# Two more PSUM banks for the dense products, and exponential and key transposes queued behind dense tiles, while gate matrices are made

## The chip, the cores and the metric

The kernel runs on one core of a Trainium2 chip. The metric is the device time of one execution in microseconds (us), as the median over several runs. TensorE is PE here (PEld is its weight load), VectorE DVE, ScalarE ACT, GpSimd POOL, and SyncE, whose queue issues most transfers, SP.

## The reference

A trunk of two layers over 512 tokens of width 1024, in float32. Layer 0 mixes by retention, layer 1 by differential attention; each is followed by a PEER expert layer, in which the gates arise:

```
q = (xc @ w_q).reshape(PEER_CHUNK, PEER_HEADS, 2, half)
sc = einsum('thpd,hpnd->thpn', q, subkeys)
s1, i1 = top_k(sc[:, :, 0], 16);  s2, i2 = top_k(sc[:, :, 1], 16)
cand = s1[..., :, None] + s2[..., None, :]      # 256 pairs of each head
top, pos = top_k(cand, 16)
idx  = expert number i1 * 128 + i2 of each chosen pair   # 8 heads x 16
gate = softmax(top)
act  = gelu(u[idx] . xc)
out  = sum over the 128 chosen experts of gate * act * v[idx]
```

There are 128 x 128 = 16384 experts, with rows `u` and `v` of 1024.

## The kernel before, in words

Products that need float32 are made of three passes (`mm3`, L95 to L98): both factors are split into a high part (`wh`, ACT, L92) and a low part (`wl`, L93, on POOL for dense tiles) and high by high, high by low and low by high are summed in PSUM.

The expert layer (`peer`, L868) treats the four blocks of 128 tokens in two ways. Block 0 is sparse: for each of its 128 chosen experts POOL gathers one row of `u` per token by an indirect transfer and DVE takes the dot product (`sparse_u`, L737), later the same with `v` (`sparse_v`, L747). Blocks 1 to 3 (384 tokens) are dense: for each of 128 groups of 128 experts a dense tile (`u_tile`, L843) computes all first products, 8 x 3 matmuls of 384 columns, and ACT takes the GELU out of the bank (L849). Gate matrices, mostly zeros, then weigh the activations, and a second product with `v` is summed over all 128 groups.

There are two stages. In the first, the one that is changed, the gate matrices are made while dense tiles run beside. The steps for a block t of 1 to 3 are:

- `topk_pairs` (L682, DVE alone): the best 16 of the candidate pairs of each head, in eight steps that each give back a cost PC = 2.2. Its last instruction, L728, subtracts the maximum: `tk_g`.
- `softmax` (L730): the exponential on ACT (L731), then sum, reciprocal and product on DVE.
- `gate_rows` (L800): DVE splits the expert number into two keys (`g_if`, L806), PE transposes both keys and the gate into one bank with the tag `rt` (L809), and DVE copies them out (`g_tr`, L811).
- `gmat` (L816): eight chunks of 16 tokens. For each four tokens DVE compares (`g_eq`, L826) and weighs (`g_oh`, L829), ACT converts (L828), PE multiplies two one-hot matrices into a `pj` bank (L833), ACT takes the result out (L836, L838). A chunk gives back a cost of 6.0 and its gates go to DRAM.

A generator, `gates()`, strings these together: the pairs of block t + 1 advance two steps after each chunk of block t, and are finished and followed by `gate_rows` at chunk 5. The loop at L920 adds up the costs that it gives back. Whenever the sum passes the dense tiles' own account, which starts at -40 and grows by UT = 4.0 per tile, it emits a tile and stores its activations to DRAM (L924). After LAG = 22 tiles it also emits sparse dot products, DOTS = 0.6 per tile, each with a cost of 1.2. In the second stage the stored tiles are loaded and weighed, and the tiles that were not made yet are made there.

What is emitted first has the higher priority. A scheduler then fixes one order for each engine before the run, with its own estimate of durations. Every engine keeps its order: an instruction that waits holds up all that stand behind it.

PSUM has eight banks: four with the tag `pj`, two `mu`, two `rt`. Dense tiles use `mu` (L845), so that a tile waits for the GELU of the tile two before it. `wh` and `wl` have three buffers. The second stage adds up in the four `pj` banks and the two `rt` banks. All loads of 128 x 1024, gathers included, go round one ring of nine buffers (`wraw`).

Of the kernel before, what the change touches and what calls it, by code (L numbers as in the profile page):

```python
# [2 lines left out]

# [20 lines left out]
AF = mybir.ActivationFunctionType  # L24
# [4 lines left out]
P = 128  # L29
S = 512  # L30
D = 1024
TB = S // P
KD = D // P
# [10 lines left out]
DT = 384  # L44

GT = 16
# [16 lines left out]
def build(tc, I, out):  # L63
    nc = tc.nc
    ctx = ExitStack()
    with ctx:
# [18 lines left out]
        XTH = xp.tile([P, KD, S], F32R, name="xth")  # L85
        XTL = xp.tile([P, KD, S], F32R, name="xtl")

        def bank(tag):
            return psum.tile([P, 512], F32, name=tag, tag=tag, bufs=4 if tag == "pj" else 2)
# [5 lines left out]
        def mm3(o, ah, al, bh, bl, start, stop):  # L95
            nc.tensor.matmul(o, ah, bh, start=start, stop=False)  # L96
            nc.tensor.matmul(o, ah, bl, start=False, stop=False)  # L97
            nc.tensor.matmul(o, al, bh, start=False, stop=stop)  # L98

        def wload(src, eng=None, pool=None, tag="", bufs=3, dst=None):  # L100
            a = src.shape[1]
            pool = pool or wp
            raw = wp.tile([P, 1024], F32, name="wraw", tag="wraw", bufs=RING)
            nc.sync.dma_start(raw.rearrange("p (a b) -> p a b", a=a), src)
            if dst is None:
                h = pool.tile([P, 1024], F32R, name="wh", tag="wh" + tag, bufs=bufs)
                l = pool.tile([P, 1024], F32R, name="wl", tag="wl" + tag, bufs=bufs)
            else:
                h, l = dst
            split(h, l, raw, eng)  # L110
            return h.rearrange("p (a b) -> p a b", a=a), l.rearrange("p (a b) -> p a b", a=a)
# [29 lines left out]
        def col_unit(b, W, q, c, ts):  # L141
            wh, wl = W
            cs = slice(c * P, c * P + P)
            for k in range(2):
                kk = 2 * q + k
                mm3(b, wh[:, k, cs], wl[:, k, cs], XTH[:, kk, ts], XTL[:, kk, ts], kk == 0, kk == 7)
# [583 lines left out]
        def softmax(gate):  # L730
            nc.scalar.activation(gate, gate, AF.Exp)  # L731
            zs = small.tile([P, 8], F32, name="tk_z", tag="tk_z")
            nc.vector.reduce_sum(out=zs, in_=gate, axis=AX.X)
            nc.vector.reciprocal(out=zs, in_=zs)
            nc.vector.tensor_tensor(out=gate, in0=gate, in1=zs.unsqueeze(2).to_broadcast([P, 8, 16]), op=OP.mult)
# [64 lines left out]
        def gate_rows(kp, idx, gate):  # L800

            ii = kp.tile([P, 2, P], I32, name="g_ii", tag="g_ii")
            nc.vector.tensor_scalar(out=ii[:, 0, :], in0=idx, scalar1=7, scalar2=None, op0=OP.arith_shift_right)
            nc.vector.tensor_scalar(out=ii[:, 1, :], in0=idx, scalar1=127, scalar2=None, op0=OP.bitwise_and)
            fi = kp.tile([P, 2, P], F32, name="g_if", tag="g_if")
            nc.vector.tensor_copy(out=fi, in_=ii)  # L806
            b = bank("rt")
            for i, src in enumerate((fi[:, 0, :], fi[:, 1, :], gate)):
                nc.tensor.transpose(b[:, i * P:i * P + P], src, ident)  # L809
            tr = kp.tile([P, 3, P], F32, name="g_tr", tag="g_tr", bufs=2)  # L810
            nc.vector.tensor_copy(out=tr.rearrange("p a b -> p (a b)"), in_=b[:, :3 * P])  # L811
            ks = kp.tile([P, 2, P], BF16, name="g_ks", tag="g_ks", bufs=2)
            nc.vector.tensor_copy(out=ks, in_=tr[:, 0:2, :])
            return tr, ks
# [25 lines left out]
                nc.sync.dma_start(gd[t0 // GT + q], st.rearrange("p a t -> p (a t)"))  # L840
                yield 6.0

        def u_tile(dp, l, a):  # L843
            uh, ul = wload(I[f"ut{l}"][a], nc.gpsimd)
            b = bank("mu")  # L845
            for k in range(KD):
                mm3(b[:, :DT], uh[:, k, :], ul[:, k, :], XTH[:, k, S - DT:], XTL[:, k, S - DT:], k == 0, k == KD - 1)
            act = dp.tile([P, DT], F32, name="uact", tag="uact", bufs=LEAD + 1)
            nc.scalar.activation(act, b[:, :DT], AF.Gelu_apprx_tanh)  # L849
            return act  # L850

        def v_prep(kp, l, a, act, g):
# [15 lines left out]
        def peer(l, norm, feed, prepare):  # L868
            with tc.tile_pool(name="sp", bufs=1) as sp, tc.tile_pool(name="dp", bufs=1) as dp:
                gd = dram.tile([DT // GT, P, (P - GA * NG0) * GT], F32, name=f"gd{l}")  # L870
# [4 lines left out]
                G0 = [dp.tile([P, DT // GT, GA, GT], F32, name="gl", tag="gl", bufs=2) for _ in range(NG0)]  # L875
                with tc.tile_pool(name="p1", bufs=1) as kp:
                    M = [kp.tile([P, 16, 16], F32, name=f"tk_m{t}") for t in range(TB)]
                    MI = [kp.tile([P, 16, 16], U32, name=f"tk_i{t}") for t in range(TB)]
                    with tc.tile_pool(name="pq", bufs=1) as qp:
                        scores(qp, M, MI, l, norm, feed)  # L880
                        if l == 0:
                            iota_f = qp.tile([P, P], F32, name="iota_f")
                            nc.sync.dma_start(iota_f, I["iota"])
                            nc.vector.tensor_copy(out=iota50,
                                                  in_=iota_f[:, :NCAND].unsqueeze(2).to_broadcast([P, NCAND, 16]))
                            nc.vector.tensor_copy(out=iota4, in_=iota_f.unsqueeze(2).to_broadcast([P, P, 4]))
                    with tc.tile_pool(name="tk", bufs=1) as tp:
                        def pairs(t, got):
                            idx = tp.tile([P, P], I32, name="tk_idx", tag="tk_idx", bufs=2)
                            gate = tp.tile([P, 8, 16], F32, name="tk_g", tag="tk_g", bufs=2)  # L890
                            yield from topk_pairs(tp, M[t], MI[t], idx, gate)
                            softmax(gate)
                            got.append((idx, gate))

                        def gates():

                            got = []
                            yield from pairs(1, got)
                            for t in range(1, TB):
                                rows = nxt if t > 1 else gate_rows(tp, got[0][0], got[0][1].rearrange("p h k -> p (h k)"))  # L900
                                if t + 1 < TB:
                                    more = pairs(t + 1, got)
                                for n, cost in enumerate(gmat(tp, *rows, (t - 1) * P, gd, G0)):
                                    yield cost
                                    if t + 1 < TB:
                                        for _ in range(2):
                                            c = next(more, None)
                                            if c:
                                                yield c
                                        if n == P // GT - 3:  # L910
                                            for c in more:
                                                yield c
                                            nxt = gate_rows(tp, got[-1][0], got[-1][1].rearrange("p h k -> p (h k)"))

                        for _ in topk_pairs(tp, M[0], MI[0], idx0, gate0):
                            pass
                        su = sparse_u(sp, 0, l, idx0, act0)
                        nu, nd, tv, tu = 0, 0, 0.0, -40.0

                        for cost in gates():  # L920
                            tv += cost
                            while tu < tv and nu < P:
                                act = u_tile(dp, l, nu)
                                nc.sync.dma_start(ad[nu], act)  # L924
                                nu += 1
                                tu += UT
                                while nd < DOTS * (nu - LAG):
                                    next(su, None)
                                    nd += 1
                                    tv += 1.2  # L930
                with tc.tile_pool(name="p2", bufs=1) as kp:
# [24 lines left out]
                    for a in range(P):  # L956
# [7 lines left out]
                        if a < nu:  # L964
                            act = kp.tile([P, DT], F32, name="aact", tag="aact", bufs=4)
                            nc.sync.dma_start(act, ad[a])
                        else:
                            act = ahead.pop(0)
# [25 lines left out]
        def to_attention():  # L994
# [5 lines left out]
            return Norm(0, 1), Feed(srcs, nc.gpsimd).fill(3)  # L1000

        nxt = peer(0, *retention(), to_attention)
        peer(1, *attention(*nxt), lambda: (Norm(1, 1, out), None))


# [60 lines left out]
```

## Time and profile before

| | |
|---|---|
| time, median of 3 runs | 3379.78 us (3376.13 to 3380.93) |
| the profiled execution's own time | 3375.29 us |
| its span | 3373.5 us |
| PE busy | 3225.8 us, 96% |
| DVE busy | 2636.5 us, 78% |
| POOL, ACT busy | 1615.7 us and 1393.4 us, 48% and 41% |
| first stage, layer 0 | about 540 to 960 us |
| first stage, layer 1 | about 2150 to 2575 us |

The span runs from the first to the last instruction. An engine that is busy for most of the span may still stand idle where it counts, so the rows are read stage by stage.

### The profile page before, as it was taken

What the parts mean: (1) busy time and instruction counts of PE and PEld (TensorE: products, weight loads), DVE (VectorE), ACT (ScalarE), POOL (GpSimd) and SP (SyncE); (2) the same over time, 40 slices, a digit from 0 to 9 for tenths busy, and PEclk for the clock granted to TensorE, in tenths of its full rate; (3) what the DMA queues carried; (4) which work ended last, traced back from release to release, by engine and by line L of the source; (5) the groups of instructions that cost most, each with busy time, mean ns of one, the idle gap of its engine ahead of it and who ended that gap; (6) DMA issues with size and microseconds to landing.
All of it is one profiled execution on the core that took longest, in us unless ns stands there. A gap on an engine that the chain in (4) does not pass through costs nothing. (4 is left out here: it accounts for less than half of the span.)

```text
span 3373.5 us, 47032 instructions
## 1 busy us (share of the span) xinstructions
PE 3225.8 (96%) x16666; PEld 2863.3 (85%) x16666; DVE 2636.5 (78%) x4593; ACT 1393.4 (41%) x2436; POOL 1615.7 (48%) x919
## 2 busy tenths in 40 slices
PE   9999999789999999999999999978999999999998
PEld 7888889789988889988888668978998888998887
DVE  4444559998868888999873665899986789989996
ACT  3233333476743333333333643337674333333332
POOL 1101335646542357778734423554454224777772
PEclk9999999899999999999999999989999999999999
DMA  5222223566689999899943202346678999989993
GB/s 212 85 85 83 87 94 125 166 210 224 249 295 335 371 327 336 310 334 327 332 145 95 73 26 90 124 151 211 219 249 270 338 346 360 332 321 334 323 330 128
DMA packets 304572, 763.36 MB, mean 226 GB/s; under 512 B 25040, under 2 KB 146256, under 8 KB 304336
## 3 DMA queue, kind: packets, MB, share of 16 engines
q1 hardware_dynamic: 230608, 491.88, 42.8%
q0 software_dynamic: 73728, 268.47, 22.3%
q8 instruction: 131, 2.15, 0.3%
q14 instruction: 105, 0.86, 0.1%
HBM read 687.37 MB, written 72.88 MB: 225 GB/s over the span
## 5 line engine op out<-in xcount | busy, mean ns | idle before, releaser
L93 POOL TENSOR_TENSOR wl<-wraw,wh 128x1024 fp32r<-128x1024 f32 x316 | 847.1, 2684 | 609.6 <-ACT wh L92 567.3
L92 ACT ACTIVATE wh<-wraw 128x1024 fp32r<-128x1024 f32 x632 | 663.6, 1055 | 670.6 <-DMA wraw<-in_ut 143.2
L96 PE MATMUL mu<-xth,wh 128*128 128x384 f32 (+1 forms) x2080 | 712.7, 343 | 40.8 <-ACT uact L849 40.8
L98 PE MATMUL mu<-xth,wl 128*128 128x384 f32 (+1 forms) x2080 | 709.3, 341 | 21.4 <-POOL wl L93 21.4
L97 PE MATMUL mu<-xtl,wh 128*128 128x384 f32 (+1 forms) x2080 | 705.9, 339 | 0.0
L93 DVE TENSOR_TENSOR wl<-wraw,wh 128x1024 fp32r<-128x1024 f32 x316 | 471.8, 1494 | 212.4 <-ACT wh L92 212.1
L741 POOL DMA_INDIRECT ug<-in_u,idx x256 | 309.2, 1208 | 521.6 <-DVE act L743 232.3
L743 DVE CUSTOM_DVE_ANT_0 scr<-ug,x 128x1024 bf16<-128x1024 f32 x256 | 367.4, 1435 | 129.7 <-DMA ug<-in_u,idx 128.7
L96 PEld LDWEIGHTS mu<-xth,wh 128*128 128x128 f32 x2080 | 399.7, 192 | 50.0 <-ACT uact L849 45.6
L92 ACT ACTIVATE wwh<-w 128x384 fp32r<-128x384 f32 x256 | 134.4, 525 | 739.2 <-DVE w L855 407.8
L98 PEld LDWEIGHTS mu<-xth,wl 128*128 128x128 f32 x2080 | 399.3, 192 | 25.5 <-POOL wl L93 25.5
L754 POOL DMA_INDIRECT vg<-in_v,idx x256 | 354.2, 1384 | 131.0 <-DVE x L756 72.4
L756 DVE SCALAR_TENSOR_TENSOR x<-vg,wgt,x 128x1024 f32<-128x1024 f32 x256 | 401.4, 1568 | 5.8 <-DMA vg<-in_v,idx 2.8
L97 PEld LDWEIGHTS mu<-xtl,wh 128*128 128x128 f32 x2080 | 400.0, 192 | 5.0
L97 PE MATMUL pj<-wl,wwh 128*128 128x512 f32 x1024 | 399.4, 390 | 0.0
L96 PE MATMUL pj<-wh,wwh 128*128 128x512 f32 x1024 | 398.8, 390 | 0.0
L98 PE MATMUL pj<-wh,wwl 128*128 128x512 f32 x1024 | 397.7, 389 | 0.0
L98 PEld LDWEIGHTS pj<-wh,wwl 128*128 128x128 f32 x1024 | 192.3, 188 | 40.8
L96 PEld LDWEIGHTS pj<-wh,wwh 128*128 128x128 f32 x1024 | 192.2, 188 | 37.0
L833 PE MATMUL pj<-g_oh 128*128 128x128 f32 x1536 | 192.6, 282 | 32.4 <-DVE g_oh L829 22.1
L97 PEld LDWEIGHTS pj<-wl,wwh 128*128 128x128 f32 x1024 | 192.2, 188 | 35.7
L833 PEld LDWEIGHTS pj<-g_oh 128*128 128x128 f32 x1536 | 186.9, 197 | 39.1 <-issue 15.8
(241 smaller groups left out, 5580.7 us busy)
## 6 DMA issues: line engine op xcount, KB each, us to landing
wraw<-in_ut SPq DMA_DIRECT2D x256, 512.0 KB, 4.4
wraw<-in_v SPq DMA_DIRECT2D x256, 512.0 KB, 6.8
gd<-g_st SPq DMA_DIRECT2D x48, 896.0 KB, 4.7
gl<-gd SPq DMA_DIRECT2D x28, 1536.0 KB, 12.8
ad<-uact SPq DMA_DIRECT2D x136, 192.0 KB, 3.9
aact<-ad SPq DMA_DIRECT2D x136, 192.0 KB, 6.0
wraw<-in_w_in SPq DMA_DIRECT2D x48, 512.0 KB, 4.1
wraw<-in_peer_w_q SPq DMA_DIRECT2D x32, 512.0 KB, 4.0
```

The lines of the kernel that those rows point to most:

```text
L92: nc.scalar.activation(h, src, AF.Copy)
L93: (eng or nc.vector).tensor_tensor(out=l, in0=src, in1=h.bitcast(F32), op=OP.subtract)
L96: nc.tensor.matmul(o, ah, bh, start=start, stop=False)
L97: nc.tensor.matmul(o, ah, bl, start=False, stop=False)
L98: nc.tensor.matmul(o, al, bh, start=False, stop=stop)
L741: nc.gpsimd.indirect_dma_start(out=u, out_offset=None, in_=I[f"u{l}"], in_offset=bass.IndirectOffsetOnAxis(ap=idx[:, j:j + 1], axis=0))
L743: nc.vector.tensor_tensor_reduce(out=scr, in0=u, in1=X[t], scale=1.0, scalar=0.0, op0=OP.mult, op1=OP.add, accum_out=act[:, j:j + 1])
L754: nc.gpsimd.indirect_dma_start(out=v, out_offset=None, in_=I[f"v{l}"], in_offset=bass.IndirectOffsetOnAxis(ap=idx[:, j:j + 1], axis=0))
L756: nc.vector.scalar_tensor_tensor(out=X[t], in0=v, scalar=w[:, j:j + 1], in1=X[t], op0=OP.mult, op1=OP.add)
L833: nc.tensor.matmul(b[:, i * P:i * P + P], oh[:, 1, i, :], oh[:, 0, i, :], start=True, stop=True)
```

## The change

Dense tiles of the first stage take banks with the tags `mu` and `rt` in turn. The softmax leaves `pairs` and is emitted by `exps()`, in which the exponential gets an edge in ACT's order to the newest dense tile's GELU. `rows()` does the same on PE: the transposes are ordered behind the newest dense tile's last matmul. Neither edge is a wait on a semaphore. For block 1 costs of 16, 8 and 4 are given back between the pairs, the exponential, the transposes and the first chunk. For blocks 2 and 3 the pairs are finished at chunk 4 (from 0), the exponential comes at chunk 5 and the transposes at chunk 6. Block 0's own softmax is left where it was.

```diff
-            nc.tensor.matmul(o, al, bh, start=False, stop=stop)
+            return nc.tensor.matmul(o, al, bh, start=False, stop=stop)
...
+        newest = {}
+
-        def u_tile(dp, l, a):
+        def u_tile(dp, l, a, tag="mu"):
             uh, ul = wload(I[f"ut{l}"][a], nc.gpsimd)
-            b = bank("mu")
+            b = bank(tag)
             for k in range(KD):
-                mm3(b[:, :DT], uh[:, k, :], ul[:, k, :], XTH[:, k, S - DT:], XTL[:, k, S - DT:], k == 0, k == KD - 1)
+                newest["mm"] = mm3(b[:, :DT], uh[:, k, :], ul[:, k, :], XTH[:, k, S - DT:], XTL[:, k, S - DT:], k == 0, k == KD - 1)
             act = dp.tile([P, DT], F32, name="uact", tag="uact", bufs=LEAD + 1)
-            nc.scalar.activation(act, b[:, :DT], AF.Gelu_apprx_tanh)
+            newest["gelu"] = nc.scalar.activation(act, b[:, :DT], AF.Gelu_apprx_tanh)
             return act
...
                             yield from topk_pairs(tp, M[t], MI[t], idx, gate)
-                            softmax(gate)
                             got.append((idx, gate))

                         def gates():

                             got = []
+
+                            def exps():
+                                with tc.issue_after(newest["gelu"].ins):
+                                    softmax(got[-1][1])
+
+                            def rows():
+                                with tc.issue_after(newest["mm"].ins):
+                                    return gate_rows(tp, got[-1][0], got[-1][1].rearrange("p h k -> p (h k)"))
+
                             yield from pairs(1, got)
+                            yield 16.0
+                            exps()
+                            yield 8.0
+                            nxt = rows()
+                            yield 4.0
                             for t in range(1, TB):
-                                rows = nxt if t > 1 else gate_rows(tp, got[0][0], got[0][1].rearrange("p h k -> p (h k)"))
-                                if t + 1 < TB:
-                                    more = pairs(t + 1, got)
-                                for n, cost in enumerate(gmat(tp, *rows, (t - 1) * P, gd, G0)):
+                                now = nxt
+                                more = pairs(t + 1, got) if t + 1 < TB else ()
+                                for n, cost in enumerate(gmat(tp, *now, (t - 1) * P, gd, G0)):
                                     yield cost
-                                    if t + 1 < TB:
-                                        for _ in range(2):
-                                            c = next(more, None)
-                                            if c:
-                                                yield c
-                                        if n == P // GT - 3:
-                                            for c in more:
-                                                yield c
-                                            nxt = gate_rows(tp, got[-1][0], got[-1][1].rearrange("p h k -> p (h k)"))
+                                    for c in (more if n == P // GT - 4 else itertools.islice(more, 2)):
+                                        yield c
+                                    if t + 1 < TB and n == P // GT - 3:
+                                        exps()
+                                    if t + 1 < TB and n == P // GT - 2:
+                                        nxt = rows()
...
-                                act = u_tile(dp, l, nu)
+                                act = u_tile(dp, l, nu, ("mu", "rt")[nu % 2])
```

## Rows read from the trace of the kernel before

**Rows 1.** The page, busy time of each engine and share of the span.
```profile
PE 3225.8 (96%) x16666; PEld 2863.3 (85%) x16666; DVE 2636.5 (78%) x4593; ACT 1393.4 (41%) x2436; POOL 1615.7 (48%) x919
```

**Rows 2.** Stretches: length, busy PE, PEld, DVE, ACT, POOL, clock, DMA, GB/s.
```profile
540.00:657.00 117.00, 94.25 (x499) 92.15 (x498) 116.91 (x411) 39.66 (x52) 68.77 (x27) 0.91 0.50 155
657.00:742.00 85.00, 70.45 (x451) 67.70 (x450) 78.10 (x110) 57.05 (x129) 46.10 (x17) 0.95 0.57 194
742.00:960.00 218.00, 209.81 (x1394) 208.88 (x1392) 175.96 (x192) 153.02 (x349) 119.38 (x54) 0.99 0.69 235
1000.00:1200.00 200.00, 200.00 (x884) 165.58 (x884) 162.82 (x243) 72.38 (x98) 54.33 (x48) 1.00 1.00 353
```

**Rows 3.** PE's waits, 540 to 657 us: total, times, longest.
```profile
PE mu L96 <- ACT uact L849: 10.8, 2, 6.9
PE mu L98 <- POOL wl L93: 4.3, 1, 4.3
PE rt L809 <- DVE g_if L806: 3.9, 1, 3.9
PE pj L833 <- DVE g_oh L829: 3.8, 1, 3.8
```

**Rows 4.** PE's waits, 657 to 742 us.
```profile
PE pj L833 <- DVE g_oh L829: 9.2, 6, 5.9
PE pj L833 <- ACT g_oh L828: 3.9, 2, 2.9
PE pj L833 <- ACT wh L92: 1.2, 1, 1.2
```

**Rows 5.** PE's waits, 2271 to 2389 us, layer 1, without its two for ACT.
```profile
PE pj L833 <- DVE g_oh L829: 5.5, 7, 1.5
PE rt L809 <- DVE g_if L806: 2.4, 1, 2.4
```

**Rows 6.** PE's waits, 742 to 950 us.
```profile
PE mu L96 <- ACT uact L849: 4.6, 3, 2.6
```

**Rows 7.** PE's waits, 2389 to 2560 us, layer 1.
```profile
PE mu L96 <- ACT uact L849: 5.2, 2, 3.0
```

**Rows 8.** Timeline of ACT: start, length, instruction, idle before it and its releaser.
```profile
595.38 0.31 ACT L731 ACTIVATE tk_g<-tk_g 128x128 f32<-128x128 f32 x1 [9.44 <-DVE tk_g L728]
...
638.55 0.31 ACT L731 ACTIVATE tk_g<-tk_g 128x128 f32<-128x128 f32 x1 [15.00 <-DVE tk_g L728]
```

**Rows 9.** Timeline of PE, 560 to 640 us.
```profile
560.81 0.69 PE L96 MATMUL mu<-xth,wh 128*128 128x384 f32 x1 [3.97 <-ACT uact L849]
...
563.85 0.34 PE L96 MATMUL mu<-xth,wh 128*128 128x384 f32 x1
...
565.45 0.33 PE L96 MATMUL mu<-xth,wh 128*128 128x384 f32 x1
...
639.00 0.66 PE L809 MATMUL rt<-ident,g_if 128*128 128x128 f32 x2 [3.85 <-DVE g_if L806]
```

**Rows 10.** Timeline of DVE, 540 to 660 us.
```profile
561.87 4.86 DVE L694 TENSOR_TENSOR tk_c<-tk_m 128x24 f32<-128x24 f32 x4
...
648.67 0.54 DVE L811 COPY g_tr<-rt 128x384 f32<-128x384 f32 x1
```

**Rows 11.** POOL's part of L93, 540 to 960 us: ns min/median/max, first and last start.
```profile
L93 POOL TENSOR_TENSOR wl<-wraw,wh x64: 2348/2442/9195, 541.2 to 949.2; 128x1024 fp32r<-128x1024 f32 x64
```

**Rows 12.** First of three passes into `mu`: 500 to 639, then 639 to 721.3 us.
```profile
L96 PE MATMUL mu<-xth,wh x174: 333/334/689, 519.8 to 634.0; 128*128 128x384 f32 x174
...
L96 PE MATMUL mu<-xth,wh x90: 331/334/687, 639.5 to 718.3; 128*128 128x384 f32 x90
```

**Rows 13.** The page, DMA issues: count, KB each, median us to landing.
```profile
ad<-uact SPq DMA_DIRECT2D x136, 192.0 KB, 3.9
```

More of the change, by code (lines that the diff above doesn't have):

```diff
@@ L1 @@
+import itertools
 import math
```

## The prediction

> **What bounds the kernel now.** I read the page first: PE is busy for 3225.8 of 3373.5 us [rows 1], so time can be won almost only where PE stands still. Then the table of stretches, which finds the place. Late in the kernel PE is full: 200.00 of 200 us, at a DMA share of 1.00 [rows 2]. In the stage where gates are made it isn't. In its first stretch PE has 94.25 of 117 us at a granted clock of 0.91 and DVE 116.91; in the second PE has 70.45 of 85 and DVE 78.10; in the third PE has 209.81 of 218 and DVE is down at 175.96. So the stage has a head that DVE bounds, a middle in which both are near full, and a tail that PE bounds. Layer 1 repeats this.
>
> Next, what PE waited for. In the head it waits 22.8 us: twice for the GELU that frees a `mu` bank, once for POOL's low half `wl`, once for the transposes' input `g_if`, once for the first one-hots [rows 3]. In the middle it waits 14.3 us, nearly all for one-hots [rows 4]; layer 1's middle has 13.0, 7.9 of it for DVE [rows 5] and for ACT the same 3.9 and 1.2. In the tail only the GELU is waited for, 4.6 us [rows 6], in layer 1 5.2 us [rows 7].
>
> ACT's timeline says why the GELU is late. The exponential stands in ACT's queue ahead of later GELUs and weight splits and waits there for DVE's subtraction: 9.44 us in one place, 15.00 in another [rows 8]. DVE is simply behind the place that the order gave it. PE's timeline shows the second price: after the wait that ended at 560.81 the nine matmuls to 563.85 start 0.34 us apart, the nine from there to 565.45 0.18 us apart [rows 9]. That is the lower of two clock levels, and it costs 3.04 - 1.60 = 1.4 us per long wait.
>
> **The change, part by part.**
>
> *Exponentials.* Before, 15 dense tiles have been emitted when the pairs of block 1 are done (costs 8 x 2.2 = 17.6, tiles every 4.0 from -40: 57.6 / 4 = 14.4). The new cost of 16 makes that 19, the 8 after it 21, the 4 after that 22. The first exponential goes behind GELU 19. Its input is there at 595.4 [rows 8]; GELU 19, in an undisturbed run of one tile per 24 x 0.178 = 4.3 us from 519.8 [rows 12], comes at about 601. So ACT no longer waits for DVE there. The other two go behind about GELU 38 and GELU 57 and wait for nothing. `gate0`'s exponential stays as it is. What stands behind each exponential on ACT (the split of the next tile, its GELU) is freed, and so are POOL and PE behind them.
>
> *Does the head get shorter?* I say no. DVE has 116.91 of 117 us there, and the same work remains. The transposes of block 1 stand on PE after 174 / 8 = 21.75 tiles [rows 12]; the new edge asks for tile 21 at least, which changes nothing. PE will reach them earlier and wait for `g_if` there, for DVE still delivers it near 639 [rows 9]. The head's 22.8 us and its five slow starts (7 us) become one wait of some 25 us, plus the first one-hots. I take a gain of 0; the bounds are 0 and 2 x 29.8 = 60 us, if the order puts the transposes of both layers late enough.
>
> *The middle.* The second transposes stand after 174 + 90 matmuls, 33 tiles, now [rows 12]. In the changed order I count 22 tiles + 4 chunks x 3.2 + 3 x 1.8 (a chunk costs 10.4 with two steps of pairs or 6.0 without, a tile 4.0 less the 0.72 that its sparse dots add), so about 40 when they are emitted. The same gate products are spread over some 19 tiles in place of 11.25. PE's work in that stretch grows from 70.45 to 70.45 + 7.75 x 4.3 = 104 us, DVE's from 78.10 to 84 if only five more dots come (1.2 each), and to 103 if each extra tile's POOL subtraction blocks it for its whole 2.44 us [rows 11]. PE is then the longer of the two, DVE catches up, and one-hot waits go. I leave 2 us a layer for the first chunks. Gains: 14.3 - 2 + 1.4 (the 5.9 us wait's slow start) = 13.7, and 13.0 - 2 = 11.0 in layer 1.
>
> *Four banks.* A dense tile no longer waits for the GELU two tiles back but four back: 8.6 us more room, against tail waits of at most 3.0 us. Gain 4.6, and 5.2 + 1.4 = 6.6 in layer 1. The bounds are 0 and this. The wait at the stage's end stays: the tiles made ahead there use `mu` alone.
>
> *Eight more tiles per layer.* The costs added are 28; with the dots 28 / 3.28 = 8.5, so 76 tiles are stored in place of 68 (the 136 stores of [rows 13] are 2 x 68). Their products move from the second stage to the first: PE's sum is the same. Added are 8 stores on SP's queue and 8 loads in the second stage, 192 KB each. The second stage moves 353 GB/s at a DMA share of 1.00 with PE full [rows 2]; the faster pace of gathers adds some 2%. I price it at 0. If that cover is gone, 2% of 76 x 4.1 us costs 6 us per layer.
>
> *The new tenant of `rt`.* The transposes hold one of the two `rt` banks until DVE copies them out: from 639.00 to 648.67 + 0.54, 10.2 us [rows 9, 10]. Nothing else wanted it. Now every other dense tile does. The banks go round, so that the tile that meets this one comes two tiles later, 8.6 us. It waits at most 1.6 us, where PE would have waited for the one-hots anyway: 0. Upper bound, if the next tile meets it: 10.2 + 1.4 per set.
>
> *Sum.* 13.7 + 11.0 + 4.6 + 6.6 = 36 us less. Against the profiled execution's 3375.29 that is 3339; its median of runs is 4.5 higher, so 3344 us.
>
> **A rule weighed against the rows.** Rows say that GELU waits are only the visible end of DVE's lateness. The Trainium skill (Perfetto Trace Analysis, section Matmuls) says that independent matmul groups should rotate through different PSUM banks, so that one group's evacuation overlaps the next group's matmuls. By it alone the GELU waits of head and tail would simply vanish, about 15 us a layer by [rows 3, 6]; by the rows the head's part comes back at `g_if`.
>
> One rule speaks against the change. In the rows, a DVE group of four operations on 24 elements took 4.86 us, and a POOL subtraction took 2.35 us at best and 9.20 at worst [rows 10, 11]. The Trainium skill (SBUF — State Buffer, section Who interferes with whom) says that a DVE operation with two SBUF inputs and a GpSimd operation that reads SBUF exclude each other for the whole instruction. The trace agrees with such blocking. What this would cost is the second rival.
>
> **The rivals.**
> 1. *All waits go* (head too): 36 + 60 = 96 us less, 3284. For it: DVE idles in the tail (176 of 218), so nothing else is full. Against: 116.91 of 117 in the head. Chance 0.14, with results between this and the forecast.
> 2. *DVE stays the bound.* Eight more POOL subtractions per layer fall into the stage and block DVE: 8 x 2.44 x 2 = 39 us, which eats the gain: 3383, about no change. It decides if DVE's middle grows past PE's 104 us. Against: DVE would need every block in full. Chance 0.12.
> 3. *Slower: the `rt` bank.* If the order gives the transposes' bank to the very next dense tile, PE stops for 10.2 + 1.4 us at each of six sets: 70 us, so 3380 - 36 + 70 = 3414. It turns the sign above 6 us per set. Against: the alternation and the round of two banks. Chance 0.14, with milder forms (3390) in it.
> 4. *The edges bind nothing*, and only the four banks work: 11 us less, 3369. Chance 0.10.
>
> **How the numbers follow.** The forecast has 0.50, its own range 3320 to 3362. A change under 0.2% (7 us) can't be told from none here. Faster: 0.50 + 0.14 + 0.10 = 0.74. Same: most of rival 2, 0.10. Slower: rival 3 and the rest of 2, 0.16. The range goes from 3290, which leaves out 0.04 at the lower end, to 3386, which leaves out 0.14 at the upper.
>
> **What would show it.** In the changed trace: no wait of ACT above 2 us at `tk_g`; one wait of 15 to 25 us on PE at the first transposes of each layer; waits on one-hots below 5 us a layer; GELU waits gone between the head and the stage's end; 152 stores of `ad`. I am wrong if the head shortens (then the transposes come later on PE than tile 22), if PE waits for DVE's `g_tr` at a dense tile in `rt`, or if one-hot waits are as long as before.

## The result, and the profile after

The changed kernel took 3400.48 us as the median of 6 runs (3398.09 to 3407.6), the kernel before 3379.73 us beside it: a ratio of 1.0061, 95% interval 1.0047 to 1.0075. It is slower by 0.6%, where 3344 us was forecast and 3386 was the end of the range.

The profiled execution is the slowest of the six, 3407.6 us with a span of 3405.8; e4 below is a second profile of the same kernel, with 3390.0. Each layer is cut at three starts that the timeline of PE shows: the head runs from the first transposes of `x` to the first gate transposes (`rt<-ident,g_if`), the rest of the first stage from there to the first second product (`pj<-wh,wwh`), then comes the second stage.

| us | tiles stored | layer 0: head, rest, stage two | layer 1: head, rest, stage two | span |
|---|---|---|---|---|
| before | 68 | 231.7, 328.9, 772.0 | 253.2, 329.1, 770.6 | 3373.5 |
| after | 77 | 239.5, 358.5, 743.4 | 259.9, 358.3, 753.6 | 3405.8 |
| e4, after again | 77 | 239.5, 358.3, 746.9 | 259.4, 358.0, 737.8 | 3390.0 |

Nine tiles per layer moved from the second stage to the first, each worth 24 x 0.178 = 4.27 us [rows 9], so 38.4 us. The heads grew by 7.8 + 6.7. The rests grew by 29.6 + 29.2 where 2 x 38.4 came in: a gain of 18, where 36 was forecast. Stage two shrank by 28.6 + 17.0 (by 25.1 + 32.8 in e4) where 77 went out: a loss of 31 (19 in e4). With 5 us elsewhere (2 ahead of the first head, 3 between the layers) this is the 32 us between the spans. So there are three errors to explain: the head, a halved gain in the rest, and stage two. One caution for stage two: after and e4 are the same kernel, and their second stages of layer 1 differ by 16 us (753.6 and 737.8).

From the page of after, answering [rows 1, 13]:

```profile
PE 3227.9 (95%) x16666; PEld 2856.8 (84%) x16666; DVE 2639.5 (78%) x4593; ACT 1394.8 (41%) x2436; POOL 1587.2 (47%) x919
...
ad<-uact SPq DMA_DIRECT2D x154, 192.0 KB
```

Its table of stretches, columns as in [rows 2], cut at this kernel's own transposes; then PE's waits from 540 to 667 us, and those from 667 to 1000 us [rows 3, 4, 6]:

```profile
540.00:667.00 127.00, 94.92 (x516) 93.27 (x515) 126.88 (x429) 37.53 (x51) 68.75 (x29) 0.88 0.45 143
667.00:780.00 113.00, 104.98 (x670) 103.50 (x669) 103.20 (x123) 75.19 (x166) 61.17 (x29) 0.97 0.67 229
780.00:1000.00 220.00, 212.34 (x1388) 210.28 (x1387) 178.54 (x186) 151.64 (x333) 116.28 (x58) 0.99 0.70 237
1000.00:1200.00 200.00, 196.82 (x878) 164.92 (x877) 166.03 (x242) 68.47 (x95) 66.66 (x54) 0.99 0.99 346
```

```profile
PE rt L810 <- DVE g_if L807: 19.4, 1, 19.4
PE rt L99 <- POOL wl L94: 10.2, 2, 7.3
PE pj L834 <- DVE g_oh L830: 1.9, 1, 1.9
...
```

```profile
PE pj L834 <- DVE g_oh L830: 6.8, 6, 2.9
PE pj L834 <- ACT g_oh L829: 4.4, 3, 2.3
PE mu L99 <- POOL wl L94: 4.1, 2, 2.3
```

GELU waits are gone, and a long wait stands at the transposes, as forecast; beside it the head's wait for `wl` has grown from 4.3 to 10.2 us. One-hot waits after the first transposes are about as long as they were: 11.2 us to 1000 us, where before has 13.1 [rows 4, 6]. And in 1000 to 1200 us, where PE had 200.00 of 200, it has 196.82.

**The head.** From one point of DVE's order to the transposes there are 301 DVE instructions in before and 301 in after, alike but for one (after has a sparse dot less and a cast more). Before, then after (stretches, same columns):

```profile
544.10:638.90 94.80, 75.95 (x404) 74.48 (x402) 94.71 (x301) 30.17 (x41) 57.30 (x21) 0.91 0.45 141
```

```profile
546.10:648.80 102.70, 72.55 (x404) 71.18 (x402) 102.61 (x301) 29.98 (x40) 55.77 (x22) 0.89 0.41 128
```

DVE hardly idles in either, and needs 7.9 us more. The durations of its operations with two inputs (`TENSOR_TENSOR` and the dots) sum to 56.0 us in before and 63.2 in after, those of all others to 59.2 and 59.6. One group shows it: four comparisons `tk_eq`, in before, then in after, each with POOL beside them (timelines of DVE and POOL):

```profile
596.27 3.68 DVE L719 TENSOR_TENSOR tk_eq<-iota,tk_pb 128x1600 bf16<-128x1600 bf16 x4
```

```profile
596.71 5.50 POOL L93 TENSOR_TENSOR wl<-wraw,wh 128x1024 fp32r<-128x1024 f32 x1 [1.53 <-ACT wh L92]
```

```profile
605.06 8.21 DVE L720 TENSOR_TENSOR tk_eq<-iota,tk_pb 128x1600 bf16<-128x1600 bf16 x4
```

```profile
605.66 2.63 POOL L94 TENSOR_TENSOR wl<-wraw,wh 128x1024 fp32r<-128x1024 f32 x1 [0.88 <-ACT wh L93]
608.57 1.41 POOL L742 DMA_INDIRECT ug<-in_u,idx  x1 [0.27 <-POOL wl L94]
609.99 2.42 POOL L94 TENSOR_TENSOR wl<-wraw,wh 128x1024 fp32r<-128x1024 f32 x1
```

In after the group is 4.53 us longer and two POOL subtractions, 5.05 us, lie in it. In before a subtraction lay beside it too, but there POOL was the one that waited: it took 5.50 us, where 2.35 is the shortest [rows 11], and the four comparisons kept their 3.68. Of all the groups of these stretches, `tk_eq` grew most, from 7.4 to 11.9 us (eight instructions); four sparse dots have a mean of 2141 ns where five had 1207. POOL's own 16 subtractions took 52.4 us before, 17 now 49.6: the two engines still get in each other's way, but the price has passed from POOL to DVE, which is the one that bounds the head. The Trainium skill (SBUF — State Buffer, section Who interferes with whom) states this exclusion; these rows agree.

**Stage two.** PE's waits of after, 1000 to 1740 us:

```profile
PE mu L99 <- POOL wl L94: 7.1, 7, 2.3
PE pj L98 <- DVE wl L94: 4.6, 3, 2.3
PE pj L97 <- ACT wwh L93: 3.2, 1, 3.2
PE pj L97 <- ACT wh L93: 2.9, 3, 1.0
```

Before, only the first kind is there, with 6.3 us, and 0.7 for a GELU. The new waits are for halves of weights (`wh`, `wl`) and of gated activations (`wwh`) that are made late. All loads go round one ring, so SP waits at a load until a buffer is free. SP's waits at L104 (L105 in after) from 1000 to 1640 us, in before and then in after:

```profile
SPq L104 <- DVE wl L93: 135.0, 44, 9.4
SPq L104 <- DVE x L756: 103.2, 38, 11.8
SPq L104 <- POOL wl L93: 69.0, 12, 8.0
```

```profile
SPq L105 <- DVE x L757: 152.6, 45, 9.3
SPq L105 <- DVE wl L94: 108.8, 38, 8.1
```

The row at the head of after's list is the sparse accumulation of `v` rows. Loads wait longer for that than before. This is a sign of the denser rows; that it is what delays PE is not shown (e14 below speaks against it). The code says why there is more of it at a time: the pace of the sparse rows, `flow` (L945, untouched by the diff), is worked out from the number of stored tiles, and 77 of them raise it from 0.3497 to 0.3604. With the planner's costs of L943 and L944, a fresh tile now takes (0.3604 x 8.24 - 1.24) / 0.524 = 3.30 rows with it in place of 3.13, a stored one 1.08 in place of 0.99.

### The profile page after: what moved, and what is told of

It is laid out like the page before. It is cut to its first block, busy times and chain, and to the rows that moved or that the text cites. A ratio compares the mean times of both kernels' runs of the same rounds, so it can differ in the third digit from the quotient of the medians.

```text
span 3405.8 us, 47080 instructions
## 1 busy us (share of the span) xinstructions
PE 3227.9 (95%) x16666; PEld 2856.8 (84%) x16666; DVE 2639.5 (78%) x4593; ACT 1394.8 (41%) x2436; POOL 1587.2 (47%) x919
## 4 chain that ended last, share of the span: by engine, by line
PE 70%; DVE 14%; issue 6%; DMA 5%; POOL 3%; ACT 1%; POOLq 0%; SPq 0%; DVEq 0%; ACTq 0%
PE pj L98 12%; PE pj L97 12%; PE pj L99 12%; PE rt L98 5%; PE mu L99 5%; PE rt L97 5%; PE rt L99 5%; PE mu L97 5%; PE mu L98 5%; PE pj L834 3%; DMA ug<-in_u,idx 2%; POOL wl L94 2%; DVE g_oh L830 2%; DMA wraw<-in_ut 1%; DVE tk_idf L726 1%
## 5 line engine op out<-in xcount | busy, mean ns | idle before, releaser
L93 ACT ACTIVATE wh<-wraw 128x1024 fp32r<-128x1024 f32 x632 | 662.7, 1054 | 557.8 <-issue 169.5
L99 PE MATMUL mu<-xth,wl 128*128 128x384 f32 (+1 forms) x1472 | 498.9, 339 | 20.2 <-POOL wl L94 20.0
L97 PE MATMUL mu<-xth,wh 128*128 128x384 f32 (+1 forms) x1472 | 497.3, 338 | 4.5 <-ACT wh L93 4.4
L98 PE MATMUL mu<-xtl,wh 128*128 128x384 f32 (+1 forms) x1472 | 495.2, 336 | 0.0
L93 ACT ACTIVATE wwh<-w 128x384 fp32r<-128x384 f32 x256 | 134.4, 526 | 651.5 <-issue 375.1
L97 PE MATMUL pj<-wh,wwh 128*128 128x512 f32 x1024 | 377.9, 392 | 16.4 <-ACT wh L93 10.1
L757 DVE SCALAR_TENSOR_TENSOR x<-vg,wgt,x 128x1024 f32<-128x1024 f32 x256 | 371.9, 1453 | 2.9
L99 PEld LDWEIGHTS mu<-xth,wl 128*128 128x128 f32 x1472 | 279.1, 190 | 31.7 <-POOL wl L94 30.5
L97 PEld LDWEIGHTS mu<-xth,wh 128*128 128x128 f32 x1472 | 279.6, 190 | 10.0 <-ACT wh L93 5.5
L98 PEld LDWEIGHTS mu<-xtl,wh 128*128 128x128 f32 x1472 | 279.5, 190 | 3.5
L94 DVE TENSOR_TENSOR wwl<-w,wwh 128x384 fp32r<-128x384 f32 x256 | 191.1, 747 | 107.3 <-ACT wwh L93 102.0
L99 PE MATMUL rt<-xth,wl 128*128 128x384 f32 (+1 forms) x640 | 217.4, 340 | 20.2 <-POOL wl L94 20.2
```

The source lines that it names most:

```text
L93: nc.scalar.activation(h, src, AF.Copy)
L94: (eng or nc.vector).tensor_tensor(out=l, in0=src, in1=h.bitcast(F32), op=OP.subtract)
L99: return nc.tensor.matmul(o, al, bh, start=False, stop=stop)
L757: nc.vector.scalar_tensor_tensor(out=X[t], in0=v, scalar=w[:, j:j + 1], in1=X[t], op0=OP.mult, op1=OP.add)
```

## The experiments

Line numbers of edits are those of the kernel edited. Ratios are to the kernel before in the same series, with 95% intervals; single runs of one kernel spread over some 20 us (before 3366.81 to 3388.34), and a stage two by up to 16 us, so that stage times of one profile are read beside the medians.

**e1, only the costs.** Before, with one line ahead of the loop over blocks:

```diff
+                            yield 28.0
```

> The kernel before with one thing of the change: a cost of 28 is given back after the pairs of block 1, so that about 77 dense tiles a layer are made and stored in the first stage in place of 68. Two mu banks, no edges. Theory A (the second stage pays for the nine tiles moved out of it: the same sparse rows are crowded into a shorter stage, and DVE, POOL and ACT fall behind PE there): the second stages shorten by only 17 to 29 us of the 37.5 us that nine tiles take, so this kernel is slower than before by 20 to 35 us, 3400 to 3415. Rival B (banks and edges cost the time in the first stage, the stored tiles nothing): within 7 us of before, 3373 to 3387.

3386.41 us, 1.0020 (1.0008 to 1.0031). Heads 231.8 and 250.6, rests 358.7 and 360.1, stage two 742.7 and 741.1. The time is rival B's, the cause is not: stage two gives 29 us back for 38, as theory A said, but the heads are not longer than before and the rests gain 16 us. That is nearly the 18 of the whole change, with two banks, no edges, and most of the GELU waits still there (PE, 645 to 998 us; before has 9.2 us from 645 to 968):

```profile
PE mu L96 <- ACT uact L849: 7.4, 5, 2.3
```

So most of the gain in the rest comes with the cost alone.

**e2, no costs.** After, without `yield 16.0`, `yield 8.0` and `yield 4.0` (68 tiles).

> The changed kernel without the costs of 16, 8 and 4: banks in turn and edges stay, about 68 tiles are stored. Theory A: the second stage is as long as before (771 us); the first loses some us in the head to DVE and POOL, which disturb each other more once ACT no longer waits, and wins some in the tail: 3365 to 3382. Rival B: about as slow as the changed kernel, 3395 to 3405.

3407.87 us, 1.0088 (1.0068 to 1.0108). This is above both ranges, and no faster pace is in it. PE comes to the transposes after 17 tiles, before the DVE work is done, and waits 22.8 us (heads 235.9 and 253.0); stage two took 780.5 and 781.3, of which a GELU wait of 4.3 us had only moved across the stage's boundary.

**e3, capped.** After, with its costs, but no more than 68 tiles in the first stage:

```diff
-                            while tu < tv and nu < P:
+                            while tu < tv and nu < 68:
```

> The changed kernel, but the first stage stops at 68 dense tiles; all else of its order stays, so that its last chunks of gates have no tile beside them. Theory A: the second stage is as long as before, and the first one's end loses up to 10 us a layer without tiles: 3375 to 3395, faster than the changed kernel. Rival B: the loss in the first stage stays and the end costs more, 3400 to 3420.

3381.57 us, 1.0008 (0.9998 to 1.0019): no change, as theory A allowed. With 68 tiles stored the pace is the old one, and the loss is gone; so is the gain. The heads are 234.3 and 259.3: with the same edges, layer 0's head grew by 2.6 us only.

**e4, the changed kernel again.**

> The changed kernel once more, for a second profile of it. Its profiled execution was 7 us above its median. If the loss lies where the first profile shows it, the first stages again come out as long as nine tiles more than before, within 3 us, and the second stages shorten by 17 to 30 us in place of 37.5.

3398.14 us, 1.0058 (1.0040 to 1.0076); the stages are in the table above. Heads and rests repeat within 0.5 us, stage two does not.

**e5, only the banks.** Before, with dense tiles of the first stage in `("mu", "rt")[nu % 2]`.

> The kernel before, with dense tiles in mu and rt banks in turn and nothing else. Theory C (whatever lets dense tiles run on while DVE makes the pairs makes POOL's subtractions fall on DVE's two-input operations and lengthens the head; the GELU waits that are won there come back at the transposes): ACT is still held by the exponentials, so the head stays within 3 us of 231.7 and 253.2 us, and the tail wins its 4.6 and 5.2 us: 3365 to 3380. Rival D (the rt bank that the transposes hold stops dense tiles): PE waits at dense tiles in rt after each transposes, 3385 to 3405.

3397.87 us, 1.0063 (1.0038 to 1.0088). The time is rival D's, but PE's only wait for `g_tr` at a dense tile of layer 0's stage is one of 0.7 us. Here too PE is at the transposes after 17 tiles and waits 17.3 us for `g_if` there; the first stages as a whole are not longer (heads 229.3 and 252.4, rests 328.6 and 333.5). The time went in stage two, 782.4 and 781.9, at an unchanged pace; in layer 0 a GELU wait of 4.3 us of it had moved across the boundary, as in e2. Why the rest was lost is not settled. With e2 this says that the pace is not all: at 0.3497 and 68 tiles, medians of 3380 (before), 3382 (e3), 3398 (e5) and 3408 us (e2) were measured.

**e6, no edges; e7, no banks.** After without the two `issue_after`; and after with all dense tiles in `mu`.

> The changed kernel without the two edges; places of emission, costs and banks stay. Theory C: the exponentials go back to GELUs 13, 20 and 23 in ACT's order, ACT waits for DVE there again, and the head is within 3 us of the one before (231.7 and 253.2); with the nine tiles' second-stage loss 3382 to 3394. Rival E (the banks alone lengthen the head): the head stays at 239 and 259 us, 3394 to 3405.

> The changed kernel with all dense tiles in mu. Theory C: the edges alone lengthen the head: 236 to 242 us and 256 to 262; GELU waits in the tail are back, some 5 us a layer: 3395 to 3410. Rival E: the head is as before, 3380 to 3392.

e6: 3389.9 us, 1.0042 (1.0025 to 1.0059), heads 231.9 and 253.0. e7: 3394.75 us, 1.0052 (1.0034 to 1.0070), heads 239.0 and 259.4. So in this kernel the edges make the head longer, by 7 us a layer, and the banks have no part in it: theory C, not E (e7 came out just under C's time).

**e8, the old pace.** After, with the pace of the kernel before:

```diff
-                    flow = (sum(load) + row * (2 * P - nd)) / (sum(time) - TAIL * time[-1])
+                    flow = 0.3497
```

> The changed kernel with the second stage's pace of sparse rows set to what the kernel before works out (0.3497 in place of 0.3604): 3.13 rows beside a dense tile of that stage in place of 3.30, and the rows end 4 tiles before the stage's end in place of 9. Theory F (the second stage loses its 8 to 13 us a layer because the rows crowd DVE there): the second stages shorten by 4 to 12 us a layer, 3375 to 3392. Rival G (rows are not it): within 4 us of the changed kernel.

3360.95 us, 0.9951 (0.9935 to 0.9968). Heads 240.0 and 259.3, stage two 732.6 and 722.8: 39 and 48 us shorter than before, all of the 38 and more, and the time lies below the ranges of both theories. SP's waits in 1000 to 1640 us, the same two kinds:

```profile
SPq L105 <- DVE wl L94: 143.2, 45, 7.2
SPq L105 <- DVE x L757: 78.4, 29, 12.3
```

The wait for the accumulation has halved against after, and PE waits 7.5 us in 1000 to 1740 in place of 17.8. One constant turns a loss of 0.6% into a gain of 0.5%. Bandwidth was not what it freed: from 1010 to 1730 us after and then e8 move 334 and 335 GB/s, and PE is 6 us busier in e8 (stretches):

```profile
1010.00:1730.00 720.00, 707.51 (x3350) 614.00 (x3349) 633.97 (x687) 253.25 (x345) 406.40 (x264) 1.00 0.94 334
```

```profile
1010.00:1730.00 720.00, 713.52 (x3401) 622.64 (x3401) 640.56 (x686) 253.88 (x347) 411.46 (x265) 1.00 0.95 335
```

**e9, the kernel before at a slower pace:** `flow = 0.3397`.

> The kernel before with its second stage's pace set to 0.3397 in place of 0.3497: 2.97 sparse rows beside a fresh tile in place of 3.13, rows that end some 4 tiles before the stage's end in place of 9. Theory H (PE is held up wherever more than about 3.1 rows stand beside a fresh tile; before sits just at that point): the second stages keep their 772 and 771 us within 5 us, 3372 to 3382. Rival I (any thinner pace wins, the change or not): the second stages shorten by 8 us and more each, 3355 to 3368, and what the changed kernel won by its old pace is not its own.

3445.87 us, 1.0202 (1.0183 to 1.0222). Stage two took 807.1 and 806.8, 35 us more each; neither theory expected that. PE's waits from 1000 to 1740 us are 28.4 us, 16.0 for DVE's `wl` and 12.4 for GELUs. SP waits mostly for POOL here, and 45.7 us for the accumulation (1000 to 1640 us):

```profile
SPq L104 <- POOL wl L93: 149.4, 27, 8.6
...
SPq L104 <- DVE x L756: 45.7, 26, 3.9
```

**e10 and e11, the old pace without edges.** e1 and e6 with `flow = 0.3497`.

> The cost of 28 alone (two mu banks, no edges), with the pace 0.3497. Head as before, second stages as with the old pace in the changed kernel (733 and 723 us): 3345 to 3362, below both kernels. If the second stage's loss does not hang on the pace alone: 3375 to 3388.

> Costs, late places of emission and four banks without the edges, with the pace 0.3497. By the theory that the edges lengthen the head by 7 us a layer: 10 to 18 us below the changed kernel with that pace (3361), 3343 to 3352. If the edges win in the rest of the stage what they lose in the head: 3356 to 3366.

e10: 3356.94 us, 0.9938 (0.9920 to 0.9956), as expected. e11: 3354.34 us, 0.9933 (0.9914 to 0.9951), between its two ranges, and the lowest median of more than one run. The pace is worth 29 us in e10 against e1, 36 in e11 against e6, 40 in e8 against after. The three at the old pace can't be told apart: beside the costs, banks and edges add nothing measurable.

**e12, a head without POOL's subtractions.** After; for the first 24 tiles of a layer ACT makes the low half, as a plain copy of the weights in place of the remainder, so that part of the computation is changed:

```diff
+            if eng == "act":
+                nc.scalar.activation(l, src, AF.Copy)
...
-            uh, ul = wload(I[f"ut{l}"][a], nc.gpsimd)
+            uh, ul = wload(I[f"ut{l}"][a], "act" if a < 24 else nc.gpsimd)
```

> The changed kernel; for the first 24 dense tiles of each layer the low part is not subtracted on POOL but is a copy that ACT makes of the loaded weights, so that POOL does no such subtraction in the head and those tiles' products are other numbers. Theory C (POOL's subtractions and DVE's two-input operations exclude each other, and the edges only let more of them meet): the same DVE instructions up to the first transposes take 100 us or less in place of 114.0, the head is 225 us or shorter. Rival J (DVE does other or more work before the transposes): DVE's sum stays above 110 us.

This is one run, and read for the head alone: 3348.96 us; heads 215.0 and 236.8, 24.5 and 23.1 us shorter than in after, though ACT does more. The stretch of the head shown above, which held 301 DVE instructions, is down to 78 us, with DVE still busy throughout:

```profile
544.23:622.30 78.07, 70.98 (x410) 70.66 (x408) 77.98 (x303) 47.38 (x58) 6.82 (x6) 0.98 0.53 175
```

In it, operations with two inputs sum to 40.1 us, the others to 57.1. The same comparisons (groups of DVE, 530 to 625 us: total, mean ns) are back at the duration that they had in before:

```profile
L723 DVE TENSOR_TENSOR tk_eq<-iota,tk_pb 128x1600 bf16<-128x1600 bf16 x8 | 7.4, 982 | 0.0
```

At the transposes PE waits 7.2 us, where after has 19.4. Stage two, at the new pace, stays at 743.1 and 743.0.

**e13 to e16, the pace as a curve.** The kernel before at 0.3604 and 0.3448, and e6 at 0.3448 and 0.3551.

> The kernel before with the pace of sparse rows that the changed kernel used (0.3604 for 0.3497), 68 stored tiles. Theory S (the second stage's time is a smooth curve of the pace, best near 0.3497): the faster pace costs here what it cost with 77 tiles, 12 to 25 us per layer, so stage two takes 783 to 796 us and the kernel 3400 to 3430. Theory J (what counts is how the rows fall between tiles in the one fixed order, and it jumps from pace to pace): anything from 3350 to 3440, with no order between it and its neighbours. Theory N (a faster pace is harmless, only the stored tiles were the cost): 3372 to 3386.

> The kernel before at a pace of 0.3448, halfway to the 0.3397 that gave 3446. Theory S: between 3380 and 3446, near 3400 to 3415. Theory J: no such order, under 3390 or over 3425 as likely as between.

> Four banks and costs without the edges, 77 stored tiles, at 0.3448 (3354 at 0.3497, 3390 at 0.3604). Theory S: the curve rises below 0.3497, 3358 to 3385. Theory J: not between its neighbours, by more than 10 us either way.

> The same at 0.3551, halfway between 0.3497 (3354) and 0.3604 (3390). Theory S: 3360 to 3382. Theory J: outside 3354 to 3390.

Median us by pace, with e6, e9 and e11:

| tiles stored | 0.3397 | 0.3448 | 0.3497 | 0.3551 | 0.3604 |
|---|---|---|---|---|---|
| 68 (before) | 3446 | 3378 | 3380 | | 3412 |
| 77 (no edges) | | 3381 | 3354 | 3358 | 3390 |

Both rows have one floor and rise on either side, as theory S said, but that the curve is smooth is not shown: e14 and e16 came out 2 us below its ranges (near 3400 to 3415 was said for e14), e14 is in what theory J allowed, and the step from 0.3448 to 0.3397 is one of 68 us. Nor is the best pace one number: the floor lies at 0.3448 to 0.3497 with 68 tiles, 0.3497 to 0.3551 with 77. e13, 1.0114 (1.0081 to 1.0146), is the shortest proof of the loss: the new pace alone, in the kernel before, costs 15 us in each stage two (787.2 and 786.1). Over these stages PE waits 19.4 and 18.3 us, where before has 7.0 and 6.7. SP's wait for the accumulation (1000 to 1640 us) is then the longest of all; but at the slower pace of e14, which loses nothing, it is as long as in after. e13, then e14:

```profile
SPq L104 <- DVE x L756: 178.2, 50, 10.9
```

```profile
SPq L104 <- DVE x L756: 148.2, 47, 9.2
```

So that wait alone does not say what PE loses.

## Why the prediction was wrong

**The step that failed: stage two at a price of 0.** "I price it at 0. If that cover is gone, 2% of 76 x 4.1 us costs 6 us per layer." The step looked at the added stores and loads and named the faster pace of gathers, but took it for 2% more traffic under the cover of a full PE. By the code the pace rises by 3%, and what it sets is how many sparse rows stand beside each dense tile on POOL and DVE, where halves of weights are made too. Measured: 15 us in each stage two from the pace alone (e13), and some 40 us between after and e8, with nothing changed but that constant. Bandwidth doesn't explain it, for the faster e8 moves as much there, 335 GB/s to after's 334. PE's rows show it standing for late halves, 17.8 us in place of 7.0 in layer 0; which queue makes them late is not settled, for SP's wait for the accumulation is as long in e14, where no time is lost. PE at 200.00 of 200 us [rows 2] was no sign that more work beside it would be free.

**The head: 0, measured +7.8 and +6.7.** The waits did move to the transposes, at the same place after about 22 tiles, one of 19.4 us where 25 was said (19.0 in layer 1). That DVE bounds the head was right. That its work "remains" was not: as many instructions, alike but for one, took 7.9 us more. The exclusion was weighed, but only for eight more subtractions in the middle. In the head it needs hardly more of them (17 for 16), only another place. e6 and e7 show that the edges do it, e12 that the subtraction is what blocks. That ACT's wait before had kept POOL off DVE at the right moment fits the rows, but was not tried by itself. Rival 2 had the mechanism, but in the middle and for 39 us; it came in the head, for 14.5.

**The middle and the tail: 36, measured 18.** The term was mis-sized: e1 has 16 of the 18 us with most GELU waits in place, so the part of the gain that rested on freed banks didn't come. ACT's waits at `tk_g` are gone, as forecast: the first exponential now starts behind a GELU without idling (timeline of ACT):

```profile
617.97 0.47 ACT L853 ACTIVATE uact<-mu 128x384 f32<-128x384 f32 x1
618.46 1.28 ACT L732 ACT_TABLE_LOAD   x1
619.75 0.31 ACT L732 ACTIVATE tk_g<-tk_g 128x128 f32<-128x128 f32 x1
```

GELU waits in the tail are gone too. One-hot waits were to fall below 5 us a layer; in 667 to 1000 us they are 6.8 for DVE and 4.4 for ACT, and in layer 1 (2275 to 2640 us) 8.6 and 5.9, where before has 5.5 and 3.9. That is the third of the prediction's own signs of being wrong. DVE's stretch has 103.20 of 113 us busy and PE 104.98: the two are still equal, where PE was to be clearly longer. The 10.2 us for `wl` in the head come from POOL's order: a gather waits for DVE, and the subtraction that PE needs stands behind it (timeline of POOL):

```profile
595.27 1.12 POOL L742 DMA_INDIRECT ug<-in_u,idx  x1 [13.07 <-DVE tk_p L708]
596.43 4.67 POOL L94 TENSOR_TENSOR wl<-wraw,wh 128x1024 fp32r<-128x1024 f32 x2
```

**The banks.** Rival 3 didn't come: after has no PE wait for `g_tr` at a dense tile in that stage (e6 has one of 2.3 us). Nor did the gain: e5 is slower than before, and e10 without the banks equals e11 with them. The Trainium skill (Perfetto Trace Analysis, section Matmuls) advises rotating banks, so that reading one out overlaps the next products. By it GELU waits were to vanish; they did, and no time came of it.

**The stores.** 152 were forecast, 154 came: nine tiles a layer, not eight.

What stays open: by which queue the faster pace makes PE wait, why the time rises on the slow side of the pace (e9), and why stage two is longer in e2 and e5 at the old one.

## What to carry to other kernels

When an edit moves a count that a planner reads, recompute everything that the planner derives from it and price that too; here one rate cost more than all the intended parts gave. A full engine in the profile is no proof that work added beside it is free: here a run with that one rate changed (e13) showed its price at once, and bytes did not. And where an engine bounds a stage, look at which other engine's work lengthens its operations before you release that one: a stall elsewhere may have been sheltering it.

## What was unexpected of the hardware

A group of DVE comparisons took 3.68 us in one order, while the POOL subtraction beside it took 5.50 in place of 2.35, and 8.21 us in another, while POOL's took 2.63 and 2.42. With no subtraction on POOL in it, the DVE-bound stretch of 102.7 us came down to 78.1 (e12). And a change of 1.5% in a software pace, from 0.3448 to 0.3397, moved the kernel before by 68 us.
